# Sixty-four more tokens by gather and three dots ahead of a transpose, in a hybrid decoder block on one core

## The chip, the cores and the metric

The kernel runs on one core of one Trainium2 chip. The metric is the device time of one execution in microseconds (us), taken as the median of several runs. The hardware profiler records one further execution, and all rows of the trace come from it. The engines are named as the profile names them: PE is TensorE (PEld its weight loads), DVE is VectorE, ACT is ScalarE, POOL is GpSimd, SP is SyncE. A q behind the name means the engine's sequencer or queue.

## What is computed

One decoder block over 1024 tokens of width 1024: an RWKV-7 branch and a sparse attention branch are merged, then comes the PEER expert mixer, to which the change belongs. Each token has 8 heads; each head scores two sets of 128 sub-keys, takes the best 16 of each, and the best 16 of their sums. So a token has 128 slots, each with one of 16,384 experts and a gate. Cut to this part:

```python
s = einsum('thcn', q, sub_keys); s1, i1 = top_k(s[:, :, 0], 16); s2, i2 = top_k(s[:, :, 1], 16)
top_s, pos = top_k(s1[..., :, None] + s2[..., None, :], 16)      # 16 experts of each of 8 heads
experts = (i1 * 128 + i2)[pos]; gates = softmax(top_s)
act = gelu(einsum('cd,chkd->chk', h2, u_tab[experts])) * gates    # u_tab, v_tab: 16384 x 1024
y2  = einsum('chk,chkd->cd', act, v_tab[experts])
x   = layer_norm(ALPHA * x + gt2 * y2, ln2_g, ln2_b)
```

## The kernel before

The PEER stage treats the tokens in two ways. **Dense tokens** (the last DN = 640) go through all 16,384 experts: 128 groups of 128 experts (index i1) are multiplied with the tokens' h2, the result goes through Gelu and is multiplied by a gate table that is zero where a token has not chosen the expert, and the products go through the second table. **Gathered tokens** (the first TD = 384, three tiles of 128, one token to a partition) fetch only their own experts' rows from HBM, one slot of all 128 tokens per indirect DMA: 128 rows of 4 KB, 512 KB in one gather step. A tile has 128 steps on table u (a product and sum on DVE, L1389, gives one dot) and 128 on table v (a multiply and add into PSUM, L1393). Three tiles are 768 steps, called rows 0 to 767 below.

- `dots_u` (L1290) is one u group of the dense tokens. `split2` (L1265) loads a 512 KB weight tile (raw), ACT copies its high part (whi), POOL computes the low part (wlo, L1271); `mm6` (L1281) multiplies with both halves of the tokens, 48 matmuls of 320 columns in all (L1284, L1286, L1288). `dense_v` (L1319) does the same for table v. There are 128 u tiles and 136 v tiles (the last eight are read twice, for tokens 0 to 383 and 384 to 639 of the dense ones, each followed by a final layer norm, `fin1`, L1445).
- 69 of the u tiles are multiplied early, while keys are still being searched (`dots_ahead`, L1642); their results go to DRAM (dotD). The last part of the program multiplies the other 59 and all 136 v tiles.
- `retrieve` (L1118) finds the keys of one tile of 128 tokens, mostly on DVE. `by_slot` (L1228) transposes what it found on PE (L1233, into slots), and `gate_table` (L1240) writes the gate table of a dense tile in 16 blocks of 8 tokens: two compares on DVE, 8 scaled copies on ACT, 8 matmuls on PE (L1258), two copies.
- `peer_gather` (L1349) is the sequence of gather steps of a tile, `finish` (L1424) its residual and layer norm. Rows 0 to 127 are issued in the second merge and before, rows 128 to 299 beside the early dots, rows 300 on (MIDDLE) beside the rest. From row 300 on a step has one of four buffers (three named g, one g2); `finish` takes four more tiles of the name g for a tile that is not the last.

Each engine works through its instructions in one fixed order. That order is decided when the program is built, by a scheduler with a model of the machine, not written out by hand; a gather step of POOL waits until DVE has used the step four before it, and a DVE instruction that waits for a gather holds all that stands behind it on DVE.

Of the kernel before, what the change touches and what calls it, by code (L numbers as in the profile page):

```python
# [42 lines left out]
XOB = 2  # L43
QIB = 2
GM = 1
GX = 3
TIES = 3
ROW0 = 8
ROW1 = 128
NG = 3  # L50
TD = NG * 128
DN = 1024 - TD
CUT = 384
PAIRS = 3
# [148 lines left out]
def body(tc, a, out, dbg=None, ntiles=8, mark=lambda s: None):  # L203
# [227 lines left out]
    for H in range(2):  # L431
# [11 lines left out]
    xaD = [tc.dram_tile([128, 1024], F32, name=f"xaD{i}") for i in range(NG)]  # L443
    h2D = [tc.dram_tile([128, 1024], F32, name=f"h2D{i}") for i in range(NG)]
    xaT = tc.dram_tile([128, 8, DN], F32, name="xaT")

    def split_act(hi, lo, src):
# [556 lines left out]
    def merge(H, y, bz, mp, side, ties):  # L1004
# [75 lines left out]
        if c0 < 512:  # L1080
            for n in range(2):
                G.dma_start(h2TD[:, n, :, dst], h2T[:, n, :, c0:])
        for tt, xn in enumerate(xns[:max(0, NG - 4 * H)]):

            i = H * 4 + tt
            for n, to in enumerate((xaD[i], h2D[i])):
                o = mp.tile([128, 1024], F32, name="xo", bufs=XOB)
                V.tensor_tensor(o, xn, rows[2 * n], op=OP.mult)
                G.tensor_tensor(o, o, rows[2 * n + 1], op=OP.add)
                nc.sync.dma_start(to, o)  # L1090
# [27 lines left out]
    def retrieve(i, keysT, tp_, then):  # L1118
# [95 lines left out]
        if i < NG:  # L1214
            ef = i1
# [65 lines left out]
    def mm6(pts, wh, wl, ah, al, k, last, halves=HALVES):  # L1281
# [3 lines left out]
        for n, h in enumerate(halves):  # L1285
            mm(pts[n], lhsT=wh, rhs=al[:, h], start=False, stop=False)  # L1286
        for n, h in enumerate(halves):
            mm(pts[n], lhsT=wl, rhs=ah[:, h], start=False, stop=last)  # L1288

    def dots_u(i1, du, h2T, bufs):  # L1290
        uh, ul = split2(du, a["ut"][i1])
# [50 lines left out]

    def gather_all(at):

        for i in range(NG):
            acc = yield from peer_gather(i, at)
            finish(i, acc, at)

    def peer_gather(i, at):  # L1349

        pg = at["pg"]

        def index(row):
            t = (gp if row < EARLY else at["du"] if row < MIDDLE else at["dv"]).tile([128, 128], U32, name="gidx")
            nc.sync.dma_start(t, idxD[i])
            return t

        def room(row):
            if EARLY <= row < MIDDLE and row % (GB + GX) >= GB:
                return at["sl"].tile([128, 1024], F32, name="gx", bufs=GX)  # L1360
# [6 lines left out]
        nc.sync.dma_start(gates, gateD[i])  # L1367
        h2 = gp.tile([128, 1024], F32, name="gh2")
        nc.sync.dma_start(h2, h2D[i])
        if i > 0:  # L1370
            hp = pg.tile([128, 1024], F32, name="pg")
            copy(hp, h2)
            h2 = hp
        dots = gp.tile([128, 128], F32, name="dots")
        for n in range(4):

            half = slice(64 * (n % 2), 64 * (n % 2) + 64)
            if n == 2:
                acc = pg.tile([128, 1024], F32, name="pg")
            for k in range(half.start, half.stop):  # L1380
                row = 64 * (4 * i + n) + k - half.start
                if idx is None or row in (EARLY, MIDDLE):
                    idx = index(row)
                u = room(row)
                G.indirect_dma_start(out=u, out_offset=None, in_=a["u" if n < 2 else "v"],  # L1385
                                     in_offset=bass.IndirectOffsetOnAxis(ap=idx[:, k:k + 1], axis=0))
                with behind(row):
                    if n < 2:
# [6 lines left out]
            if n < 2:  # L1395
# [27 lines left out]

    def finish(i, acc, at):  # L1424

        last = i == NG - 1
# [3 lines left out]
        V.tensor_tensor(y2, acc, row, op=OP.mult)  # L1430
        nc.sync.dma_start(xa, xaD[i])
        V.tensor_tensor(y2, y2, xa, op=OP.add)
# [4 lines left out]
        out_rows(i * 128, 128, (y2[:, 0:512], y2[:, 512:1024]), y2, g, b, gp.tile([128, 16], F32, name="lnst"), last)  # L1437

    def fin_rows(du):
        ln, dst = (du.tile([128, 2, 1024], F32, name="gt", bufs=2) for _ in range(2))  # L1440
# [20 lines left out]

    slots = {}

    def by_slots(i, f):
        if i >= NG:
            slots[i] = tk.tile([128, 3, 128], F32, name="slots", bufs=2)
            by_slot(f, slots[i])

    qTD = [tc.dram_tile([128, 8, 512], F32, name=f"qTD{i}") for i in range(2)]
    h2TD = tc.dram_tile([128, 2, 8, DN], F32R, name="h2TD")  # L1470
# [15 lines left out]
    for H in range(2):  # L1486
# [127 lines left out]
    with tc.tile_pool(reuse_waits=REUSE, name="du", bufs=1) as du, \  # L1614
# [6 lines left out]
        with tc.tile_pool(reuse_waits=REUSE, name="slots", bufs=1) as sl, \  # L1621
# [8 lines left out]
                    by_slots(i, f)  # L1630
                found[i] = gate_table(i, slots[i], sl, du, st, keys8)

            for i in slots:
                table(i)
            side = retrieve_all(range(M1, 8), tk, table)
            more = {"du": du, "sl": sl, "pg": pg}
            rows = gather_all(more)
# [9 lines left out]
                    yield  # L1647

            ahead_ = dots_ahead()

            def beside(tables, dots, n):

# [81 lines left out]
```

## Time and profile before

| what | value |
|---|---|
| median of 3 runs | 3749.42 us (3740.57 to 3751.53) |
| the profiled execution's own time | 3743.65 us |
| its span, first to last instruction | 3741.9 us |
| PE busy | 3505.2 us (94%) |
| DVE, ACT, POOL busy | 2596.4 (69%), 1695.7 (45%), 1981.3 us (53%) |
| moved by the DMA engines | 920.95 MB, mean 246 GB/s |

The span is the time between the first and the last instruction; the profiled execution's own time is 1.75 us longer. Matmuls are pipelined, so their durations overlap, and the distance between starts tells the pace. The granted clock (PEclk) is the share of full speed that TensorE got. From 1677 us on PE works on the dense tokens, first with the gate tables between the dots, then without.

### The profile page before, as it was taken

What the parts mean: (1) busy time and instruction counts of PE and PEld (TensorE: products, weight loads), DVE (VectorE), ACT (ScalarE), POOL (GpSimd) and SP (SyncE); (2) the same over time, 40 slices, a digit from 0 to 9 for tenths busy, and PEclk for the clock granted to TensorE, in tenths of its full rate; (3) what the DMA queues carried; (4) which work ended last, traced back from release to release, by engine and by line L of the source; (5) the groups of instructions that cost most, each with busy time, mean ns of one, the idle gap of its engine ahead of it and who ended that gap; (6) DMA issues with size and microseconds to landing.
All of it is one profiled execution on the core that took longest, in us unless ns stands there. A gap on an engine that the chain in (4) does not pass through costs nothing.

```text
span 3741.9 us, 64784 instructions
## 1 busy us (share of the span) xinstructions
PE 3505.2 (94%) x24045; PEld 3139.0 (84%) x24045; DVE 2596.4 (69%) x5433; ACT 1695.7 (45%) x3230; POOL 1981.3 (53%) x1572
## 2 busy tenths in 40 slices
PE   8999999889999999869999999999999999999997
PEld 7677777666677777649999989999999999999997
DVE  7756653857467775899999985376777767676754
ACT  3549953243344443447667678322223322222223
POOL 5452222354455553245655532467677667677755
PEclk9999999989999999889999999999999999999998
DMA  7463323864676666378988864898999989989963
GB/s 231 137 171 103 107 87 123 290 196 161 214 220 219 215 212 218 115 250 317 335 308 316 309 240 171 292 333 322 334 330 331 323 319 327 340 320 325 333 225 123
DMA packets 436880, 920.95 MB, mean 246 GB/s; under 512 B 36452, under 2 KB 195508, under 8 KB 433876
## 3 DMA queue, kind: packets, MB, share of 16 engines
q1 hardware_dynamic: 311956, 498.38, 39.8%
q0 software_dynamic: 124608, 418.43, 31.4%
q8 instruction: 189, 3.10, 0.3%
q14 instruction: 127, 1.04, 0.1%
HBM read 791.59 MB, written 125.08 MB: 245 GB/s over the span
## 4 chain that ended last, share of the span: by engine, by line
PE 49%; DVE 14%; DMA 13%; issue 8%; POOL 7%; ACT 6%; SPq 0%; POOLq 0%; ACTq 0%; DVEq 0%
PE pair L1284 7%; PE pair L1286 7%; PE pair L1288 7%; PE acc L423 4%; PE acc L424 4%; PE acc L425 4%; POOL g L1385 3%; DMA g<-in_u_dram,gidx 3%; DMA raw<-in_vt_dram 3%; POOL wlo L1271 3%; DMA g<-in_v_dram,gidx 3%; PE tp L1258 2%; DMA raw<-in_ut_dram 2%; ACT gt L232 2%; PE acc L975 2%
## 5 line engine op out<-in xcount | busy, mean ns | idle before, releaser
L1271 POOL TENSOR_TENSOR wlo<-raw,whi 128x1024 fp32r<-128x1024 f32 x264 | 643.8, 2440 | 388.9 <-ACT whi L232 367.5
L413 POOL TENSOR_TENSOR wlo<-wraw,whi 128x512 fp32r<-128x512 f32 x280 | 371.3, 1329 | 557.3 <-ACT whi L232 505.9
L232 ACT ACTIVATE whi<-raw 128x1024 fp32r<-128x1024 f32 x264 | 278.9, 1057 | 681.1 <-PE pair L1286 320.7
L1385 POOL DMA_INDIRECT g<-in_u_dram,gidx x361 | 373.6, 1035 | 298.4 <-DVE g L1389 180.5
L1284 PE MATMUL pair<-A,whi 128*128 128x320 f32 (+2 forms) x2048 | 482.1, 312 | 25.6 <-DVE A L1316 18.3
L1393 DVE SCALAR_TENSOR_TENSOR pg<-g,dots,pg 128x1024 f32<-128x1024 f32 x317 | 407.1, 1284 | 123.1 <-DMA g<-in_v_dram,gidx 118.0
L1286 PE MATMUL pair<-A,whi 128*128 128x320 f32 (+2 forms) x2048 | 481.2, 311 | 0.2 <-DVE A L1316 0.2
L1288 PE MATMUL pair<-A,wlo 128*128 128x320 f32 (+2 forms) x2048 | 480.4, 311 | 0.6 <-POOL wlo L1271 0.6
L1288 PE MATMUL pair<-h2T,wlo 128*128 128x320 f32 x2048 | 474.3, 312 | 2.1 <-POOL wlo L1271 2.1
L1284 PE MATMUL pair<-h2T,whi 128*128 128x320 f32 x2048 | 475.6, 312 | 0.2 <-ACT ds L232 0.2
L1286 PE MATMUL pair<-h2T,whi 128*128 128x320 f32 x2048 | 473.3, 311 | 0.0
L1385 POOL DMA_INDIRECT g<-in_v_dram,gidx x320 | 307.7, 961 | 170.8 <-DVE pg L1393 80.8
L423 PE MATMUL acc<-big,whi 128*128 128x512 f32 x864 | 356.5, 413 | 18.6 <-DVE zs L531 6.8
L1284 PEld LDWEIGHTS pair<-A,whi 128*128 128x128 f32 x2048 | 349.1, 190 | 28.2 <-issue 19.1
L1389 DVE SCALAR_TENSOR_TENSOR g<-g,pg 128x1024 f32<-128x1024 f32 x233 | 281.0, 1216 | 118.4 <-DMA g<-in_u_dram,gidx 116.8
L425 PE MATMUL acc<-big,wlo 128*128 128x512 f32 x864 | 351.6, 407 | 2.3 <-POOL wlo L413 2.3
L424 PE MATMUL acc<-big,whi 128*128 128x512 f32 x864 | 349.5, 404 | 3.1 <-DVE big L449 3.1
L1288 PEld LDWEIGHTS pair<-A,wlo 128*128 128x128 f32 x2048 | 349.1, 190 | 0.8 <-POOL wlo L1271 0.8
L1286 PEld LDWEIGHTS pair<-A,whi 128*128 128x128 f32 x2048 | 349.2, 190 | 0.7 <-DVE A L1316 0.7
L1288 PEld LDWEIGHTS pair<-h2T,wlo 128*128 128x128 f32 x2048 | 343.8, 189 | 3.5 <-POOL wlo L1271 2.6
L1284 PEld LDWEIGHTS pair<-h2T,whi 128*128 128x128 f32 x2048 | 344.6, 189 | 1.6 <-ACT ds L232 0.4
L1286 PEld LDWEIGHTS pair<-h2T,whi 128*128 128x128 f32 x2048 | 343.9, 189 | 1.0
(482 smaller groups left out, 6682.5 us busy)
## 6 DMA issues: line engine op xcount, KB each, us to landing
raw<-in_vt_dram SPq DMA_DIRECT2D x136, 512.0 KB
raw<-in_ut_dram SPq DMA_DIRECT2D x128, 512.0 KB
gtD<-st SPq DMA_DIRECT2D x20, 2048.0 KB
gt<-gtD SPq DMA_DIRECT2D x32, 1280.0 KB
wraw<-in_wz_dram SPq DMA_DIRECT2D x152, 256.0 KB
dotD<-ds SPq DMA_DIRECT2D x69, 320.0 KB
al<-dotD SPq DMA_DIRECT2D x69, 320.0 KB
mw<-in_wada_dram SPq DMA_DIRECT2D x32, 512.0 KB
```

Of the source, the lines that this page charges most:

```text
L232: copy = lambda o, i, **k: A.activation(o, i, AF.Copy, **k)
L413: G.tensor_tensor(lo, raw, hi.bitcast(F32), op=OP.subtract)
L423: mm(pt, lhsT=wh[:, ks], rhs=ah[:, k, :], start=k == 0, stop=False)
L424: mm(pt, lhsT=wh[:, ks], rhs=al[:, k, :], start=False, stop=False)
L425: ins = mm(pt, lhsT=wl[:, ks], rhs=ah[:, k, :], start=False, stop=k == nk - 1)
L1271: G.tensor_tensor(lo, raw, hi.bitcast(F32), op=OP.subtract)
L1284: mm(pts[n], lhsT=wh, rhs=ah[:, h], start=k == 0, stop=False)
L1286: mm(pts[n], lhsT=wh, rhs=al[:, h], start=False, stop=False)
L1288: mm(pts[n], lhsT=wl, rhs=ah[:, h], start=False, stop=last)
L1385: G.indirect_dma_start(out=u, out_offset=None, in_=a["u" if n < 2 else "v"], in_offset=bass.IndirectOffsetOnAxis(ap=idx[:, k:k + 1], axis=0))
L1389: V.scalar_tensor_tensor(u, u, 1.0, h2, op0=OP.mult, op1=OP.mult, accum_out=dots[:, k:k + 1])
L1393: V.scalar_tensor_tensor(acc, u, dots[:, k:k + 1], acc, op0=OP.mult, op1=OP.add)
```

## The change

Sixty-four tokens (number 384 to 447, the first half of tile 3) are gathered instead of dense. DN becomes 576, so a dense matmul has 288 columns instead of 320 (and 384 and 192 instead of 384 and 256 in the last eight v tiles read twice). The 64 tokens take two partitions each, with 64 slots in each, so their gather is 64 steps on u and 64 on v, all on 128 partitions: 896 rows instead of 768. `finish` adds the two partitions of a token with a matmul against a 0/1 matrix. Tile 3's gate table has 8 blocks instead of 16. XR takes the place of the old constant GX (three early buffers).

Beside that, what the second merge finds for tile 3 is kept (`keep`) and not transposed there; the transposes are put behind three dots (FIRST). Cut to its core:

```diff
+FIRST = 3
+XR = 3
-TD = NG * 128
+GX = 64
+TD = NG * 128 + GX
+NGT = NG + (GX > 0)
...
-        for tt, xn in enumerate(xns[:max(0, NG - 4 * H)]):
+        for tt, xn in enumerate(xns[:max(0, NGT - 4 * H)]):
...
-        for b in range(16):
+        for b in range(max(0, TD - i * 128) // 8, 16):
...
-        for i in range(NG):
+        for i in range(NGT):
             acc = yield from peer_gather(i, at)
             finish(i, acc, at)
...
+        tokens = 128 if i < NG else GX
+        slots_ = tokens
+        halves = 2 if i < NG else 1
...
-        for n in range(4):
+        for n in range(2 * halves):
...
+            sel = gp.tile([128, 1024], F32, name="gh2")[:, 0:n]
+            V.tensor_reduce(sel, ident.rearrange("p (s t) -> p t s", t=n), axis=AX.X, op=OP.add)
+            copy(y2, acc)
+            acc = at["pg"].tile([128, 1024], F32, name="pg")
+            for h in range(2):
+                hs = slice(512 * h, 512 * h + 512)
+                mm(acc[p, hs], lhsT=sel, rhs=y2[:, hs], start=True, stop=True)
...
-                side = retrieve_all(range(1, M1), tk, by_slots)
+                side = retrieve_all(range(1, M1), tk, keep)
...
-            for i in slots:
-                table(i)
...
             ahead_ = dots_ahead()
+
+            for _ in range(FIRST):
+                next(ahead_)
+            for i, f in early_found.items():
+                with tc.issue_after(latest[0].ins):
+                    by_slots(i, f)
+                table(i)
```

On PE, where the last matmuls of the second merge (acc) are followed by the transposes of tile 3 (tp<-ident), stood before:

```order
L425 MATMUL acc<-Q,wlo 128x512
L1233 MATMUL tp<-ident,i_15675 128x128
L1233 MATMUL tp<-ident,gates 128x128
L1233 MATMUL tp<-ident,i_15674 128x128
L1128 MATMUL tp<-keysT,qT 128x128 x4
L1284 MATMUL pair<-h2T,whi 128x320 x2
```

and at the two ends of the same place stands now (L428 is the old L425, L1287, L1289 and L1291 are the dots, L1236 the transposes):

```order
L428 MATMUL acc<-Q,wlo 128x512
L1287 MATMUL pair<-h2T,whi 128x288 x2
L1289 MATMUL pair<-h2T,whi 128x288 x2
...
L1291 MATMUL pair<-h2T,wlo 128x288 x2
L1236 MATMUL tp<-ident,i_15685 128x128
L1236 MATMUL tp<-ident,gates 128x128
L1236 MATMUL tp<-ident,i_15684 128x128
L1131 MATMUL tp<-keysT,qT 128x128 x2
```

The three transposes moved behind 71 rows of dots, that is behind the 144 matmuls of three weight tiles.

On DVE the program ended before with the layer norm of the last dense tokens; its last gather step (L1393) stood 39 rows ahead of the end, among the last dense products (yacc):

```order
L1393 SCALAR_TENSOR_TENSOR pg<-g_36500,dots,pg 128x1024
L1330 SCALAR_TENSOR_TENSOR yacc<-pair,modc,yacc 128x640 x3
...
L1330 SCALAR_TENSOR_TENSOR yacc<-pair,modc,yacc 128x256 x7
L1404 BN_STATS lnst<-pair 128x6 x4
L1405 BN_AGGR lnst<-lnst 128x2 x2
L1407 RECIPROCAL lnst<-lnst 128x1 x2
L1410 SCALAR_TENSOR_TENSOR lnst<-lnst 128x1 x2
L1414 TENSOR_TENSOR gt<-gt 128x512 x4
```

Now the layer norm of the last dense tokens (L1426) is followed by gather steps: 9 of table v for tile 2, then tile 2's `finish` (L1445 and on), 64 of table u (L1401), the Gelu's product (L1409), 64 of table v (L1405) and the last `finish`:

```order
L1426 TENSOR_TENSOR gt<-gt 64x512 x2
L1405 SCALAR_TENSOR_TENSOR pg<-g_36306,dots,pg 128x1024
L1405 SCALAR_TENSOR_TENSOR pg<-g,dots,pg 128x1024 x3
...
L1445 TENSOR_TENSOR gacc<-pg,g 128x1024
L1457 TENSOR_TENSOR gacc<-gacc,g 128x1024
...
L1401 SCALAR_TENSOR_TENSOR g,dots<-g,pg 128x1024 x3
...
L1409 TENSOR_TENSOR dots<-dots,ggate 128x64
L1403 TENSOR_SCALAR pg<-g,dots 128x1024
```

137 gather steps moved behind the last instruction of the dense tokens, where there was none.

On POOL, between the low parts of two weight tiles in the middle of the last stage (g from in_u_dram are gather steps), stood before:

```order
L1271 TENSOR_TENSOR wlo<-raw,whi 128x1024
L1385 DMA g<-in_u_dram,gidx 128x1024 x3
L1271 TENSOR_TENSOR wlo<-raw,whi 128x1024
L1385 DMA g_35799<-in_u_dram,gidx 128x1024
L1385 DMA g<-in_u_dram,gidx 128x1024 x2
L1271 TENSOR_TENSOR wlo<-raw,whi 128x1024
```

and stands now:

```order
L1274 TENSOR_TENSOR wlo<-raw,whi 128x1024
L1397 DMA g_35617<-in_u_dram,gidx 128x1024
L1397 DMA g<-in_u_dram,gidx 128x1024
L1274 TENSOR_TENSOR wlo<-raw,whi 128x1024
L1397 DMA g<-in_u_dram,gidx 128x1024 x2
L1274 TENSOR_TENSOR wlo<-raw,whi 128x1024
```

Counted over all rows of POOL from weight tile 80 to weight tile 240, 441 gather steps stood there before (319 to 760) and 382 stand there now (313 to 695): 2.76 and 2.39 for each weight tile. The last eight v tiles that are read twice (16 tiles, 249 to 264) had no gather step beside them; now 35 DVE gather steps stand among their products and layer norms.

## Rows read from the trace of the kernel before

**Rows 1.** Busy time by stage: length, busy us (instructions) by engine, clock, DMA share, GB/s.

```profile
1640.00:1677.00 37.00, 5.99 (x29) 4.37 (x27) 31.79 (x86) 10.52 (x14) 19.93 (x18) 0.60 0.86 302
1677.00:2384.00 707.00, 681.00 (x4850) 667.02 (x4851) 573.00 (x1298) 496.33 (x1009) 356.06 (x237) 0.99 0.78 284
2384.00:3616.00 1232.00, 1211.84 (x8190) 1209.21 (x8189) 865.47 (x1055) 345.01 (x423) 851.77 (x638) 0.99 0.91 325
3657.00:3736.00 79.00, 63.52 (x425) 62.60 (x423) 38.45 (x62) 27.01 (x35) 48.76 (x25) 0.91 0.34 117
```

**Rows 2.** Waits of PE, 2420 to 3660 us: us in total, times, longest.

```profile
PE pair L1284 <- DVE A L1316: 18.3, 8, 4.3
```

**Rows 3.** Timeline of DVE: start, us, operation [idle before]; last gather step, last instructions.

```profile
3615.05 1.28 DVE L1393 SCALAR_TENSOR_TENSOR pg<-g,dots,pg 128x1024 f32<-128x1024 f32 x1
...
3731.00 4.70 DVE L1414 TENSOR_TENSOR gt<-gt 128x512 f32<-128x512 f32 x4 [0.76 <-ACT gt L1413]
```

**Rows 4.** Timeline of PE: matmuls of 320 columns, the first of 384, two of 256.

```profile
3628.70 0.46 PE L1284 MATMUL pair<-h2T,whi 128*128 128x320 f32 x2
...
3656.86 0.34 PE L1284 MATMUL pair<-A,whi 128*128 128x384 f32 x1
...
3702.05 0.29 PE L1284 MATMUL pair<-A,whi 128*128 128x256 f32 x1
...
3704.94 0.28 PE L1284 MATMUL pair<-A,whi 128*128 128x256 f32 x1
```

**Rows 5.** Busy time by stage of line L1258 alone: PE, PEld, then as in Rows 1.

```profile
1677.00:2384.00 707.00, 161.70 (x1280) 154.21 (x1280) 0.99 0.78 284
```

**Rows 6.** Timeline of PE: the transposes of tile 3 and the first dot.

```profile
1674.93 0.45 PE L1233 MATMUL tp<-ident,i 128*128 128x128 f32 x1 [31.01 <-DVE i L1193]
...
1676.89 0.90 PE L1284 MATMUL pair<-h2T,whi 128*128 128x320 f32 x2
```

**Rows 7.** Timeline of POOL: load of h2T, low parts of the first two weight tiles.

```profile
1654.72 2.79 POOL L1618 DMA_DIRECT2D h2T<-h2TD  x4 [1.00 <-issue]
1657.53 4.64 POOL L1271 TENSOR_TENSOR wlo<-raw,whi 128x1024 fp32r<-128x1024 f32 x2
```

**Rows 8.** DMA, 1650 to 1675 us, eight loads and six gather steps of POOL among it.

```profile
DMA packets 3677, 9.82 MB, mean 393 GB/s; under 512 B 290, under 2 KB 546, under 8 KB 3676
```

**Rows 9.** Timeline of POOL in the first merge: one add of xo.

```profile
763.50 2.38 POOL L1089 TENSOR_TENSOR xo<-xo,big 128x1024 f32<-128x1024 f32 x1 [6.10 <-DVE xo L1088]
```

**Rows 10.** Groups on DVE, 2384 to 3742 us: busy us, mean ns, idle before by releaser.

```profile
L1393 DVE SCALAR_TENSOR_TENSOR pg<-g,dots,pg 128x1024 f32<-128x1024 f32 x254 | 326.4, 1285 | 122.4 <-DMA g<-in_v_dram,gidx 118.0 <-DVE pg L1393 0.7 <-DVE A L1316 0.6
L1389 DVE SCALAR_TENSOR_TENSOR g<-g,pg 128x1024 f32<-128x1024 f32 x212 | 256.0, 1216 | 117.5 <-DMA g<-in_u_dram,gidx 115.9
```

**Rows 11.** Timeline of POOL: two gather steps after a pause.

```profile
3595.68 0.95 POOL L1385 DMA_INDIRECT g<-in_v_dram,gidx  x1
3596.93 0.94 POOL L1385 DMA_INDIRECT g<-in_v_dram,gidx  x1 [0.30 <-issue]
```

**Rows 12.** Timeline of DVE: the use of the first of these two.

```profile
3600.38 1.29 DVE L1393 SCALAR_TENSOR_TENSOR pg<-g,dots,pg 128x1024 f32<-128x1024 f32 x1 [3.09 <-DMA g<-in_v_dram,gidx]
```

**Rows 13.** Timeline of DVE around the finish of tile 1, inside the dense stretch.

```profile
2944.35 1.29 DVE L1393 SCALAR_TENSOR_TENSOR pg<-g,dots,pg 128x1024 f32<-128x1024 f32 x1 [0.71 <-DMA g<-in_v_dram,gidx]
...
2967.49 1.22 DVE L1389 SCALAR_TENSOR_TENSOR g<-g,pg 128x1024 f32<-128x1024 f32 x1
```

**Rows 14.** Timeline of DVE: from a last u step to the next step, past Gelu.

```profile
2444.03 1.22 DVE L1389 SCALAR_TENSOR_TENSOR g<-g,pg 128x1024 f32<-128x1024 f32 x1
...
2448.24 1.21 DVE L1389 SCALAR_TENSOR_TENSOR g<-g,pg 128x1024 f32<-128x1024 f32 x1
```

**Rows 15.** Timeline of DVE and POOL: begin and end of the last finish.

```profile
3660.85 1.22 DVE L1430 TENSOR_TENSOR gacc<-pg,A 128x1024 f32<-128x1024 f32 x1
...
3674.43 1.30 POOL L1415 TENSOR_TENSOR gacc<-gacc,gt 128x512 f32<-128x512 f32 x1 [0.63 <-DVE gacc L1414]
```

**Rows 16.** Timeline of POOL: the last instruction before the last store.

```profile
3731.77 6.26 POOL L1415 TENSOR_TENSOR gt<-gt 128x512 f32<-128x512 f32 x4 [10.08 <-DVE gt L1414]
```

More of the change, by code (lines that the diff above doesn't have):

```diff
@@ L45 @@
 GM = 1
-GX = 3
+FIRST = 3
+XR = 3
 TIES = 3
@@ L442, in body @@
         ybD[H] = tc.dram_tile([8, 128, 512], F32, name=f"ybD{H}")
-    xaD = [tc.dram_tile([128, 1024], F32, name=f"xaD{i}") for i in range(NG)]
-    h2D = [tc.dram_tile([128, 1024], F32, name=f"h2D{i}") for i in range(NG)]
+    xaD = [tc.dram_tile([128, 1024], F32, name=f"xaD{i}") for i in range(NGT)]
+    h2D = [tc.dram_tile([128, 1024], F32, name=f"h2D{i}") for i in range(NGT)]
     xaT = tc.dram_tile([128, 8, DN], F32, name="xaT")
@@ L1213, in retrieve @@
         V.tensor_tensor(gv, gv, gs[:, :, None].to_broadcast([128, 8, 16]), op=OP.mult)
-        if i < NG:
-            ef = i1
+        if i < NGT:
+            ef = i1 if i < NG else tp_.tile([128, 128], F32, name="ef")
             V.scalar_tensor_tensor(ef, i1, 128.0, i2, op0=OP.mult, op1=OP.add)
@@ L1287, in mm6 @@
         for n, h in enumerate(halves):
-            mm(pts[n], lhsT=wl, rhs=ah[:, h], start=False, stop=last)
+            latest[:] = [mm(pts[n], lhsT=wl, rhs=ah[:, h], start=False, stop=last)]
     def dots_u(i1, du, h2T, bufs):
@@ L1343, in gather_all, with rows_in @@
     def gather_all(at):
-        for i in range(NG):
+        for i in range(NGT):
             acc = yield from peer_gather(i, at)
             finish(i, acc, at)
+    def rows_in(dst, src, n, c):
+        for r in range(128 // n):
+            at = 0 if src.shape[1] == c else r * c
+            nc.sync.dma_start(dst[r * n:r * n + n, 0:c], src[0:n, at:at + c])
     def peer_gather(i, at):
         pg = at["pg"]
+        tokens = 128 if i < NG else GX
+        slots_ = tokens
+        halves = 2 if i < NG else 1
         def index(row):
             t = (gp if row < EARLY else at["du"] if row < MIDDLE else at["dv"]).tile([128, 128], U32, name="gidx")
-            nc.sync.dma_start(t, idxD[i])
+            rows_in(t, idxD[i], tokens, slots_)
             return t
         def room(row):
-            if EARLY <= row < MIDDLE and row % (GB + GX) >= GB:
-                return at["sl"].tile([128, 1024], F32, name="gx", bufs=GX)
+            if EARLY <= row < MIDDLE and row % (GB + XR) >= GB:
+                return at["sl"].tile([128, 1024], F32, name="gx", bufs=XR)
             if row >= MIDDLE and row % (GB + GM) >= GB:
@@ L1366, in peer_gather @@
         gates = gp.tile([128, 128], F32, name="ggate")
-        nc.sync.dma_start(gates, gateD[i])
+        rows_in(gates, gateD[i], tokens, slots_)
         h2 = gp.tile([128, 1024], F32, name="gh2")
-        nc.sync.dma_start(h2, h2D[i])
+        rows_in(h2, h2D[i], tokens, 1024)
         if i > 0:
@@ L1374, in peer_gather @@
         dots = gp.tile([128, 128], F32, name="dots")
-        for n in range(4):
-            half = slice(64 * (n % 2), 64 * (n % 2) + 64)
-            if n == 2:
+        for n in range(2 * halves):
+            half = slice(0, slots_) if halves == 1 else slice(64 * (n % 2), 64 * (n % 2) + 64)
+            if n == halves:
                 acc = pg.tile([128, 1024], F32, name="pg")
@@ L1384, in peer_gather @@
                 u = room(row)
-                G.indirect_dma_start(out=u, out_offset=None, in_=a["u" if n < 2 else "v"],
+                G.indirect_dma_start(out=u, out_offset=None, in_=a["u" if n < halves else "v"],
                                      in_offset=bass.IndirectOffsetOnAxis(ap=idx[:, k:k + 1], axis=0))
                 with behind(row):
-                    if n < 2:
+                    if n < halves:
                         V.scalar_tensor_tensor(u, u, 1.0, h2, op0=OP.mult, op1=OP.mult, accum_out=dots[:, k:k + 1])
@@ L1394, in peer_gather @@
                 yield
-            if n < 2:
+            if n < halves:
                 A.activation(dots[:, half], dots[:, half], AF.Gelu)
@@ L1424, in finish @@
     def finish(i, acc, at):
-        last = i == NG - 1
+        last = i == NGT - 1
+        n = 128 if i < NG else GX
+        p = slice(0, n)
         row, xa = ((at["dv"].tile([128, 2 * DN], F32, name="A", bufs=AB)[:, 0:1024] if last else grow()) for _ in range(2))
@@ L1429, in finish @@
         y2 = gp.tile([128, 1024], F32, name="gacc")
-        V.tensor_tensor(y2, acc, row, op=OP.mult)
-        nc.sync.dma_start(xa, xaD[i])
-        V.tensor_tensor(y2, y2, xa, op=OP.add)
+        if n == 128:
+            V.tensor_tensor(y2, acc, row, op=OP.mult)
+        else:
+            sel = gp.tile([128, 1024], F32, name="gh2")[:, 0:n]
[5 more added lines that the diff above has]
+                mm(acc[p, hs], lhsT=sel, rhs=y2[:, hs], start=True, stop=True)
+            V.tensor_tensor(y2[p], acc[p], row[p], op=OP.mult)
+        nc.sync.dma_start(xa[p], xaD[i][p])
+        V.tensor_tensor(y2[p], y2[p], xa[p], op=OP.add)
         g, b = at["ln"][0:2] if last else (grow(), grow())
@@ L1436, in finish @@
             rowb(b, "ln2b")
-        out_rows(i * 128, 128, (y2[:, 0:512], y2[:, 512:1024]), y2, g, b, gp.tile([128, 16], F32, name="lnst"), last)
+        out_rows(i * 128, n, (y2[:, 0:512], y2[:, 512:1024]), y2, g, b, gp.tile([128, 16], F32, name="lnst"), last)
     def fin_rows(du):
@@ L1462, in body @@
     slots = {}
+    early_found = {}
     def by_slots(i, f):
@@ L1467, in by_slots, with keep @@
             by_slot(f, slots[i])
+    def keep(i, f):
+        if i >= NG:
+            early_found[i] = f
     qTD = [tc.dram_tile([128, 8, 512], F32, name=f"qTD{i}") for i in range(2)]
```

## The prediction

> **What bounds the kernel now.** I read the busy time by stage first [rows 1]. There the reader is to see that from 1677 us on PE hardly rests: 681.0 of 707 us while the keys are searched and the gate tables built, 1211.8 of 1232 us beside the gather steps, at a granted clock of 0.99. The DMA share in the long stretch is 0.91, with 325 GB/s, so the transfers are close behind PE. Then the waits of PE in that stretch: only 18.3 us in all go to products that come late from DVE [rows 2]. Then the end of DVE's timeline: the last gather step starts at 3615.05 and the dense tokens' layer norm ends at 3731.00 + 4.70 = 3735.7 us [rows 3]. So gathering is done 120 us before the dense tokens, and whatever shortens PE's work before that point shortens the kernel, until the gather steps become the later of the two. The change pulls both ways: fewer columns on PE, 128 more gather steps.
>
> **What PE saves.** In the timeline of PE 192 matmuls of 320 columns lie between 3628.70 and 3656.86, so 146.7 ns each; 24 of 256 columns lie between 3702.05 and 3704.94, so 120.4 ns [rows 4]. No row has 288 columns. The two prices bound it; I take the middle, 133.5 ns, as 288 is the middle of 256 and 320. That saves 13.1 ns a matmul, 0.630 us for a weight tile of 48.
> - 69 early dots: 43.5 us. DVE would be the cover that fails here: it is busy 573 of 707 us [rows 1], and loses little, so it still fits into the 647 us that remain.
> - 59 other u tiles and 120 whole v tiles: 179 x 0.630 = 112.8 us.
> - The eight half tiles of 256 columns that now have 192: 192 matmuls by 26.2 ns, 5.0 us; 0 if a shorter matmul waits for its weights.
> - Eight blocks less of tile 3's table: L1258 has 1280 matmul records in 80 blocks and 161.7 us [rows 5], so 2.02 us a block, 16.2 us.
>
> **What the moved transposes save.** PE sat idle for 31.01 us until tile 3's keys were there at 1674.93, and the first dot started at 1676.89 [rows 6]. Three dots of 6.4 us could fill 19.2 us of it. But they need h2T, whose load POOL has issued by 1657.5, and low parts of weights, the second of which is ready at 1662.2 [rows 7]. The load is 5.2 MB and the DMA engines move 393 GB/s there [rows 8], so 13.3 us from 1651, and I expect the first dot near 1665: 12 us earlier, of which I count 10. The bounds are 0 (the dots wait for something else) and 19. Behind the transposes wait tile 3's table and the key matmuls of tile 4; they come later by the rest of the third dot, and DVE has gather steps to do meanwhile.
>
> **What is added ahead of the tail.** One more tile of xo in the first merge: two adds on POOL of 2.38 us [rows 9], with the weights' low parts queued behind them. Bounds 0 and 4.8; I take 2. The last double-read tiles, 79 us at 117 GB/s [rows 1] or 9.2 MB, get 35 gather steps beside them, 18.4 MB more. At 325 GB/s the 27.6 MB take 85 us, at 393 they take 70, against 74 of PE's work; I add 6 us (0 to 11). In the long stretch nothing is added: 2.39 gather steps now go with a tile of 6.41 us where 2.76 went with 7.04, so weights and gathers together ask for 277 GB/s where they asked for 280.
>
> The dense tokens would then end 43.5 + 112.8 + 5.0 + 16.2 + 10 - 2 - 6 = 179.5 us earlier, at 3556.2.
>
> **The tail, which is new.** 137 gather steps stand on DVE behind the last instruction of the dense tokens, so none of their DVE work can be hidden. One step costs DVE 1.285 us on table v and 1.216 on u [rows 10]. POOL issues two 1.25 us apart [rows 11]. A transfer of 524,288 bytes takes 1.33 us at 393 GB/s [rows 8]. So 1.33 us is the lower bound of a step. But there are four buffers, and the way round one of them is longer: 4.70 us from the issue at 3595.68 to the use at 3600.38 [rows 11, 12], 1.29 for the use, 0.30 until POOL issues again: 6.29 us, a quarter of which is 1.57 us. The upper bound is the pace of the long stretch, 468 steps in 1232 us [rows 1] or 2.63 us; but there the order ties the steps to the weight tiles. I take 1.57, because the row that it comes from has a weight load beside it and little else: 137 x 1.57 = 215.1 us.
> - Tile 2's finish now stands in the tail, with its four tiles named g. In tile 1's finish 23.14 us passed from the last v step at 2944.35 to the fourth u step at 2967.49 [rows 13]; less four steps of 1.57 that is 16.9 us.
> - Gelu between u and v: 4.21 us from the last u step to the next step [rows 14], less one step, say 3 us.
> - The last finish: 14.9 us from 3660.85 to the end of its last add [rows 15], partly shared with dense work, a copy and two matmuls for the pairs (2 us, estimated), and 3.9 us from POOL's last end at 3738.03 to the end of the span [rows 16]: 20 us.
>
> 215.1 + 16.9 + 3 + 20 = 255 us, so the span ends at 3811.2 instead of 3741.9, 69.3 us later. The profiled execution's own time was 3743.65, which gives 3813 us; that run lies 0.15% below the median of the runs shown, 3749.42. What PE saves comes back as a tail in which PE has nothing to do.
>
> **The rivals.** *A shorter way round.* With no weight load beside it a transfer may land sooner than 4.70 us after its issue, down to 1.33 us a step: 182.2 instead of 215.1 us, 3780 us in all. The early stage speaks for it, with 393 GB/s over 25 us [rows 8]; against it, that no gather there was used at once. A rule of the Trainium skill leads the same way: "DMA: Bandwidth & Descriptors", section "Anatomy of one DMA — SWDGE (gpsimd) path", fits a transfer from POOL's path as 2.0 us plus its bytes over 436 GB/s, 3.2 us for a gather step. With issue and use that would be an estimate of 1.44 us a step and 3795 us; the row's 4.70 us, less the issue of 0.95, is 3.75 and so above it.
>
> *A slower tail.* If a transfer of random rows keeps the way that it has beside the weights, the step stays at 2.0 to 2.63 us, 3872 to 3958 us. The 118 and 116 us for which DVE waited for gathers [rows 10] speak for it; that the order set the pace there speaks against. The same side takes the case that gathers hold PE up in the long stretch, since DVE's products stand behind them.
>
> *Faster.* PE's price falls by more than I think. To end 0.3% lower, at 3732 us, the dense tokens must end 81 us earlier still; over 248 whole tiles of 48 matmuls that is 6.8 ns each, so 288 columns would have to cost below 126.7 ns, near the 120.4 of 256. The tail alone can't do it: it would need steps of less than 1 us, and DVE alone needs 1.22.
>
> *The transposes bring nothing:* 10 us more, inside the range.
>
> **How the numbers follow.** My forecast (step of 1.45 to 1.75 us, 3797 to 3838) gets 0.62, the shorter way round 0.18, the slower tail 0.14, faster 0.03, no change 0.03 (a fast step and a larger gain together). A difference of 0.3%, 11 us, is about what a measurement of this kernel can tell from no change. The range leaves out the two last cases, most of the slower tail and the lowest edge of the short one: 3768 to 3862.
>
> **What would show it.** Right: dots of 288 columns 133 ns apart; PE's idle time before the transposes gone, dots from about 1665; the last product of the dense tokens near 3556; behind it some 250 us with PE almost idle, DVE's steps 1.5 to 1.7 us apart, each waiting for its gather, and POOL waiting for DVE. Wrong: PE waits of far more than 18 us for DVE's products in the long stretch (the gathers hold PE); steps 1.3 or 2 us apart in the tail; or a tail that starts much before or after 3556.

## The result, and the profile after

The changed kernel takes 3915.06 us (median of four runs, 3897.85 to 3920.95), the kernel before 3750.48 beside it: ratio 1.0433, interval 1.04 to 1.0465, so slower. The forecast was 3813 us, 3768 to 3862; slower came true, the size did not. The profiled execution took 3897.85 us with a span of 3895.7, 84.5 us behind the span that the prediction adds up to.

The page of the changed kernel: busy time, then DMA packets.

```profile
PE 3364.8 (86%) x23921; PEld 2994.4 (77%) x23921; DVE 2739.8 (70%) x5625; ACT 1650.8 (42%) x3156; POOL 2102.5 (54%) x1702
...
DMA packets 448418, 977.19 MB, mean 251 GB/s; under 512 B 42036, under 2 KB 190084, under 8 KB 445668
```

Busy time by stage, columns as in [rows 1]: a piece of the dense stretch, its end, two of the tail.

```profile
2600.00:2800.00 200.00, 198.38 (x1486) 197.82 (x1485) 139.61 (x143) 58.86 (x75) 141.92 (x104) 1.00 0.92 333
...
3500.00:3600.00 100.00, 81.72 (x501) 79.35 (x500) 69.60 (x81) 27.08 (x33) 82.23 (x61) 0.89 0.89 305
3600.00:3700.00 100.00, 6.68 (x50) 6.14 (x49) 74.98 (x105) 5.86 (x9) 52.48 (x54) 0.53 0.83 282
3700.00:3850.00 150.00, 0.00 (x0) 0.00 (x0) 105.86 (x119) 0.26 (x1) 77.80 (x84) 0.50 0.87 293
```

Up to 3500 us it looks like [rows 1]. Then comes the tail: PE has nothing to do and its granted clock stands at 0.5, the lower of the two levels; the DMA share is a little lower than beside the dense tokens, 0.83 to 0.87 in place of 0.92, and no other engine is full.

Timeline of POOL: the 301st, the 768th and the 896th, last gather. In the kernel before the 301st stands at 2384.50, the 768th and last at 3605.86.

```profile
2357.79 0.95 POOL L1397 DMA_INDIRECT g<-in_u_dram,gidx  x1 [7.17 <-DMA gidx<-idxD]
...
3631.71 0.94 POOL L1397 DMA_INDIRECT g<-in_v_dram,gidx  x1 [2.23 <-DVE pg L1405]
...
3868.05 0.94 POOL L1397 DMA_INDIRECT g<-in_v_dram,gidx  x1 [0.53 <-DVE pg L1405]
```

These rows give the time as one chain of gathers. From the 301st gather to the 768th are 467 steps: 1221.4 us before (2.615 each), 1273.9 after (2.728). Then 128 steps in 236.3 us (1.846 each, finish of tile 2 and Gelu included), then 27.6 us to the end of the span. The gathers, which were done 120 us ahead of the dense tokens [rows 3], now end last.

Timeline of DVE: the end of the dense tokens' last layer norm, which answers to the second row of [rows 3], with a v step behind it.

```profile
3617.90 5.20 DVE L1426 TENSOR_TENSOR gt<-gt 128x512 f32<-128x512 f32 x3
3623.02 3.92 DVE L1405 SCALAR_TENSOR_TENSOR pg<-g,dots,pg 128x1024 f32<-128x1024 f32 x3
```

3623.1 against 3735.7: 112.6 us earlier, where 179.5 were forecast.

PE's waits from 1650 to 2380 us, after; in the kernel before, the four that answer were 11.5, 0, 2.1 and, beside the single idle time of 31.0, 8.7.

```profile
PE tp L1261 <- ACT st L235: 21.9, 16, 3.7
PE pair L1287 <- ACT whi L235: 18.1, 3, 11.2
PE pair L1291 <- POOL wlo L1274: 17.2, 12, 3.8
PE tp L1236 <- DVE i L1196: 5.5, 3, 1.9
```

The tail itself on table u, POOL and then DVE: a gather, the step whose end freed its buffer, and the step that uses it.

```profile
3702.58 0.93 POOL L1397 DMA_INDIRECT g<-in_u_dram,gidx  x1 [1.83 <-DVE g L1401]
```
```profile
3701.08 1.22 DVE L1401 SCALAR_TENSOR_TENSOR g<-g,pg 128x1024 f32<-128x1024 f32 x1 [1.53 <-DMA g<-in_u_dram,gidx]
...
3708.06 1.22 DVE L1401 SCALAR_TENSOR_TENSOR g<-g,pg 128x1024 f32<-128x1024 f32 x1 [1.14 <-DMA g<-in_u_dram,gidx]
```

POOL waits for DVE to free a buffer, DVE for the gather to land, here 6.98 us for one way round, 5.48 of it from issue to use. The median over gathers 775 to 825, pairing the nth gather with the nth step, is 5.47; with 1.22 for the use and 0.28 until the next issue a buffer's way round is 6.97 us, a quarter of it 1.74, and the issues from the 775th to the 825th follow each other 1.733 us apart.

### The profile page after: what moved, and what is told of

It is laid out like the page before. It is cut to its first block, busy times and chain, and to the rows that moved or that the text cites. A ratio compares the mean times of both kernels' runs of the same rounds, so it can differ in the third digit from the quotient of the medians.

```text
span 3895.7 us, 65006 instructions
## 1 busy us (share of the span) xinstructions
PE 3364.8 (86%) x23921; PEld 2994.4 (77%) x23921; DVE 2739.8 (70%) x5625; ACT 1650.8 (42%) x3156; POOL 2102.5 (54%) x1702
## 5 line engine op out<-in xcount | busy, mean ns | idle before, releaser
L1397 POOL DMA_INDIRECT g<-in_u_dram,gidx x425 | 434.5, 1022 | 341.7 <-DVE g L1401 211.0
L1405 DVE SCALAR_TENSOR_TENSOR pg<-g,dots,pg 128x1024 f32<-128x1024 f32 x380 | 488.1, 1285 | 158.9 <-DMA g<-in_v_dram,gidx 146.9
L1287 PE MATMUL pair<-A,whi 128*128 128x288 f32 (+2 forms) x2048 | 460.3, 302 | 35.5 <-DVE A L1319 24.4
L1397 POOL DMA_INDIRECT g<-in_v_dram,gidx x384 | 365.8, 953 | 231.3 <-DVE pg L1405 128.3
L1401 DVE SCALAR_TENSOR_TENSOR g<-g,pg 128x1024 f32<-128x1024 f32 x297 | 358.3, 1216 | 161.4 <-DMA g<-in_u_dram,gidx 158.7
L1291 PE MATMUL pair<-h2T,wlo 128*128 128x288 f32 x2048 | 452.5, 301 | 17.2 <-POOL wlo L1274 17.2
L1287 PE MATMUL pair<-h2T,whi 128*128 128x288 f32 x2048 | 451.4, 301 | 18.3 <-ACT whi L235 18.1
L1291 PE MATMUL pair<-A,wlo 128*128 128x288 f32 (+2 forms) x2048 | 458.2, 301 | 4.8 <-POOL wlo L1274 4.8
L1289 PE MATMUL pair<-A,whi 128*128 128x288 f32 (+2 forms) x2048 | 458.4, 301 | 1.9 <-DVE A L1319 1.9
L1289 PE MATMUL pair<-h2T,whi 128*128 128x288 f32 x2048 | 447.7, 300 | 0.0
L1287 PEld LDWEIGHTS pair<-A,whi 128*128 128x128 f32 x2048 | 341.7, 193 | 39.1 <-issue 26.2
L1291 PEld LDWEIGHTS pair<-h2T,wlo 128*128 128x128 f32 x2048 | 335.6, 192 | 21.1 <-POOL wlo L1274 20.0
L1287 PEld LDWEIGHTS pair<-h2T,whi 128*128 128x128 f32 x2048 | 335.9, 192 | 20.7 <-ACT whi L235 19.1
L428 PE MATMUL acc<-big,wlo 128*128 128x512 f32 x864 | 349.4, 405 | 2.3 <-POOL wlo L416 2.3
L1291 PEld LDWEIGHTS pair<-A,wlo 128*128 128x128 f32 x2048 | 341.6, 193 | 5.5 <-POOL wlo L1274 5.5
L1289 PEld LDWEIGHTS pair<-A,whi 128*128 128x128 f32 x2048 | 342.0, 193 | 2.5 <-DVE A L1319 2.5
L1289 PEld LDWEIGHTS pair<-h2T,whi 128*128 128x128 f32 x2048 | 335.8, 192 | 0.7
```

What stands on the lines that cost most here:

```text
L428: ins = mm(pt, lhsT=wl[:, ks], rhs=ah[:, k, :], start=False, stop=k == nk - 1)
L1287: mm(pts[n], lhsT=wh, rhs=ah[:, h], start=k == 0, stop=False)
L1291: latest[:] = [mm(pts[n], lhsT=wl, rhs=ah[:, h], start=False, stop=last)]
```

## The experiments

All are compared with the kernel before on the same chip. Four kernels asked first whether PE's pace carries through.

**The move alone.**

```diff
-GX = 64
+GX = 0
```

> The move of the transposes alone: 384 tokens are gathered and 640 stay dense, as before the change; the last keys found in the second merge are transposed behind three dots. Theory of the prediction (up to the dense stage PE sets the pace, so what PE gains at the start of the early stage is kept to the end): the 10 to 24 us that PE gains at the first dots pass through, 3727 to 3740 us. Rival (the early stage ends with its last gate table, which follows DVE and ACT, so a gain of PE alone is lost in a wait ahead of the dense stage): no gain, 3745 to 3755 us.

3743.23 us, ratio 0.9985 (0.9971 to 0.9999): 6 us, between the two theories. The first dot starts at 1656.44 instead of 1676.89 [rows 6], but PE's last dense matmul is only 11 us earlier.

**The gathers alone.**

```diff
-FIRST = 3
+FIRST = 0
-                side = retrieve_all(range(1, M1), tk, keep)
+                side = retrieve_all(range(1, M1), tk, by_slots)
-            for i, f in early_found.items():
-                with tc.issue_after(latest[0].ins):
-                    by_slots(i, f)
+            for i in list(slots):
                 table(i)
```

> The 64 more gathered tokens alone: the transposes stay in the second merge's place, ahead of every dot. Theory of the prediction (PE's pace counts to the end): later than the changed kernel by what the move gave, 10 to 24 us, so 3920 to 3940 us. Rival (the early stage ends with the last gate table): the same as the changed kernel within 6 us, 3900 to 3921 us, and the wait ahead of the dense stage shorter by 10 to 24 us than the changed kernel's 38 us.

3907.25 us, 1.0421 (1.04 to 1.0441): the same as with the move. The first dot is 37 us later than in the changed kernel, PE's last dense matmul 6 us, and the time not at all. So the slowdown comes with the 64 tokens alone, and the move neither helps nor harms it.

**75 early dots instead of 69.** In the changed kernel the early dots run out at 2296 us, and until 2331 PE has only table matmuls, in lots that wait for ACT (14.2 us in all).

```diff
-EXTRA = 10
+EXTRA = 16
```

> The changed kernel with 75 dots computed ahead in place of 69. Rival (PE stands idle ahead of the dense stage because the early dots run out before the last gate table is written and read back): the six dots, some 30 us of PE at 48 matmuls each, fill the idle time of about 38 us and are missing later from the dense stage, so the dense stage ends 22 to 32 us earlier and the time is 3870 to 3893 us. Theory of the prediction (PE sets the pace throughout): the dots only change their place, 3898 to 3921 us.

3911.33 us, 1.0441 (1.0418 to 1.0464): no gain. This is the run that settles most. Its PE timeline shows where the dense tokens' transposes begin, 3605.20 in the changed kernel:

```profile
3570.97 0.71 PE L1477 MATMUL pair<-ident,yacc 128*128 128x128 f32 x5
```

No table matmul waits for ACT in this kernel from 2230 to 2360 us, and PE is done 34 us earlier, as the rival said, although this profile's first dot starts 9 us later (the changed kernel's profile is the shortest of its runs). But the time stays; the theory of the prediction has the time right and the reason wrong. The gathers end where they did: the 301st is issued at 2376.63, the 768th at 3630.89 and the last at 3873.85. The program's order, which is made anew for every version, now leaves 155 steps behind the last instruction of the dense tokens, where it left 137, so what PE gains only lengthens the tail.

**The move with 75 dots**, 384 tokens gathered.

```diff
-EXTRA = 10
+EXTRA = 16
-GX = 64
+GX = 0
```

> The move alone, 384 tokens gathered, with 75 dots computed ahead in place of 69. Rival (the move's gain is lost ahead of the dense stage where the early dots run out): the added dots give it back, 3722 to 3738 us, while the move with 69 dots stays at 3745 to 3755. Theory of the prediction: the same as the move with 69 dots, 3727 to 3740 us.

3742.11 us, 0.9973 (0.9959 to 0.9986): of the versions that compute every row the only one that, with the move alone, lies below both kernels, by 0.27%. It can't be told from the move alone, and its own profiled execution took 3751.27.

Next came the gathers.

**Two more buffers.**

```diff
-GM = 1
+GM = 3
```

> The changed kernel with six gather buffers in place of four from row 300 on. Theory A (a step of the last stretch lasts a quarter of the way from a gather's issue round to the buffer's next use, 5.3 to 6.3 us and more over four buffers): with six buffers a step comes below 1.5 us, and the 126 steps behind the last dense token give back 35 us or more, 3845 to 3880 us. Theory B (the DMA engines themselves pass one 512 KB gather in about 1.79 us, whatever stands in line): the step stays at 1.7 to 1.8 us, the time from issue to use grows to 8 us or more, 3895 to 3920 us.

3791.32 us, 1.0113 (1.009 to 1.0136): 124 us off, more than either theory allowed, on the side of theory A. Busy time of the gathers alone (POOL), in 1000 us beside the dense tokens and in 50 us of the tail: length, busy us (gathers), clock, DMA share, GB/s. The changed kernel:

```profile
2450.00:3450.00 1000.00, 340.68 (x362) 0.99 0.89 323
3700.00:3750.00 50.00, 25.95 (x28) 0.50 0.88 297
```

With six buffers, the tail once in the same 50 us and once behind the dense tokens' layer norm, which lasts to 3714 here:

```profile
2450.00:3450.00 1000.00, 391.76 (x415) 0.98 0.95 345
3700.00:3750.00 50.00, 30.87 (x33) 0.50 0.95 357
3720.00:3760.00 40.00, 28.34 (x31) 0.50 1.02 399
```

The tail alone shows theory A: the last 35 steps are 1.325 us apart, where four buffers took 1.73 to 1.80, and issue to use is 6.4 us, not the 8 and more of theory B. DVE rests no more; its timeline has 14 steps in 18.5 us:

```profile
3714.08 18.50 DVE L1405 SCALAR_TENSOR_TENSOR pg<-g,dots,pg 128x1024 f32<-128x1024 f32 x14
```

Beside the dense tokens there are 415 gathers in place of 362, but not by the buffers alone. With six buffers the program's order itself has 2.88 gather steps for each weight tile from tile 80 to tile 240, counted as in the section on the change, instead of 2.39; which of the two made the pace, no run separates. The last gather is issued 106 us sooner, at 3762.0. But PE now pays for it; its waits from 2460 to 3500 us, six buffers:

```profile
PE pair L1291 <- POOL wlo L1274: 40.1, 31, 2.6
PE pair L1287 <- ACT whi L235: 22.4, 14, 5.5
```

In the changed kernel the row that answers to [rows 2] leads, and no wait for weights is listed:

```profile
PE pair L1287 <- DVE A L1319: 22.1, 10, 4.4
```

So 62.5 us of waiting for weights, where there was none, and PE's last dense matmul comes at 3697 instead of 3605. Followed back to what came late, some 45 of the 62.5 us end at the load of a weight tile, and some 11 at gather steps that stand ahead of a low part on POOL.

**Without the fourth tile's gathers.**

```diff
-        for i in range(NGT):
+        for i in range(NG):
-        last = i == NGT - 1
+        last = i == NG - 1
```

> The changed kernel without the gathers of the fourth tile: the expert mixing of the 64 tokens and their 64 output rows are left out, 576 tokens stay dense, and 768 gathers remain. Theory of the prediction (PE sets the pace to the end of the dense tokens): 3565 to 3590 us. Rival (from the dense stage on, weights and gathers share the DMA engines, and the 768th gather is issued at 3630 us behind PE's end at 3605 us): the third tile's finish ends it, 3650 to 3680 us, so the 128 gathers of the fourth tile alone cost 230 to 260 us.

3667.14 us, 0.9784 (0.9764 to 0.9804). The 128 gathers cost 248 us, and with 768 gathers the fewer dense tokens give only 79 us against the kernel before (3746.54 beside it): the rival. PE is done at 3622, the last gather step at 3651.

**Sixty rows ahead of the dense stage**, in the stretch in which the DMA engines idle.

```diff
-MIDDLE = 300
+MIDDLE = 360
-            n = (MIDDLE - EARLY) // (steps + 6)
+            n = (300 - EARLY) // (steps + 6)
```

Rows 300 to 359 then also take the six early buffers (g and gx) of the rows ahead of them.

> The changed kernel with 60 more gathered rows (300 to 359) ahead of the dense stage, behind the last retrieval, where the DMA engines are busy for 0.54 of 2200 to 2300 us and no gather runs from 2218 to 2358 us. Theory of the gather stream (behind row 300 the end is the number of gathers left, each at its DMA time): up to 60 steps of 1.79 us are saved, less what the added DVE steps cost the last gate tables, 3800 to 3850 us. Theory of the prediction (the dense stage's end and then a tail): the 60 rows shorten the tail too, but the added DVE work holds up the tables that PE waits for, so 3830 to 3880 us.

3836.87 us, 1.024 (1.0221 to 1.0258), inside both forecasts. It saves 78 us although one row of PE shows what the added steps cost, the dense tokens' first products behind them on DVE:

```profile
2414.67 0.82 PE L1287 MATMUL pair<-h2T,whi 128*128 128x288 f32 x2 [43.35 <-DVE A L1319]
```

**All three together.**

```diff
-EXTRA = 10
+EXTRA = 16
-MIDDLE = 300
+MIDDLE = 360
...
-GM = 1
+GM = 3
...
```

The second mark stands for the line on n, as with the sixty rows, here and in all kernels below that change MIDDLE.

> The changed kernel with the three edits together: 60 rows ahead of the dense stage, six gather buffers from there on, 75 dots computed ahead. Theory of the gather stream with the DMA engines as its limit: no better than the 60 rows alone within 10 us, 3790 to 3850 us, since dots and buffers move no byte. Theory A (buffers limit the last stretch): 40 us or more below the 60 rows alone. In neither is it below the kernel before at 3750 us.

3796.24 us, 1.0112 (1.0087 to 1.0137). That is 41 us below the sixty rows alone, as theory A wanted, but no better than the two buffers alone, so rows and dots add nothing to them; the first product is again 35.1 us late.

**Five buffers and seven.**

```diff
-GM = 1
+GM = 2
```

> The changed kernel with five gather buffers from row 300 on (four gave 3915 us, six 3791). Theory A (the way round a buffer over the number of buffers sets the step): a step of the last stretch goes from 1.8 us to about 1.45, of the dense stretch from 2.78 to about 2.5, and the time lies between, 3825 to 3865 us. Theory A with the DMA engines' limit met already at five: 3785 to 3810 us.

3852.41 us, 1.0269 (1.0252 to 1.0287), in the range of theory A. Gathers alone, five buffers:

```profile
2450.00:3450.00 1000.00, 351.19 (x372) 1.00 0.91 329
3700.00:3750.00 50.00, 31.11 (x34) 0.50 0.96 347
```

In the tail 34 gathers in place of 28: steps of 1.52 us, between the 1.73 to 1.80 of four buffers and the 1.325 of six. The DMA share of 0.96 looked like a limit and was none, for the sixth buffer brought 399 GB/s in place of 347.

```diff
-GM = 1
+GM = 4
```

> The changed kernel with seven gather buffers from row 300 on. If the DMA engines are the limit at six (they were busy for 0.95 to 0.98 of the dense stretches, and a gather's way from issue to use had grown from 7.1 to 11 us): no better than six, 3775 to 3805 us, the way longer again by about a sixth. If buffers still set the step: 20 us or more below six, 3735 to 3770 us.

3794.44 us, 1.0122 (1.0102 to 1.0142): no better than six, as the DMA engines' limit would have it. Gathers alone, and then PE's waits from 2460 to 3500 us, seven buffers:

```profile
2450.00:3450.00 1000.00, 409.35 (x434) 0.95 0.95 347
```
```profile
PE pair L1291 <- POOL wlo L1274: 64.8, 54, 3.6
PE pair L1287 <- ACT whi L235: 43.9, 15, 8.7
```

The DMA share and the rate are those of six; 19 more gathers come through in 1000 us (3.34 steps a weight tile in the program's order), and PE waits 108.7 us for weights, some 66 of them for a load. The gathers are done at 3724, PE at 3775: the last place has changed hands, and the time has not.

**Six buffers without the fourth tile's gathers.**

```diff
-GM = 1
+GM = 3
-        for i in range(NGT):
+        for i in range(NG):
-        last = i == NGT - 1
+        last = i == NG - 1
```

> Six gather buffers and no gathers of the fourth tile: the expert mixing of the 64 tokens and their output rows are left out. The gathers then end near 3510 us and PE's end sets the time. Theory of the prediction (the dense stage is PE's alone): 3580 to 3615 us, some 55 to 85 below the four buffers without the fourth tile at 3667. Rival (weights and gathers share the DMA engines, and faster gathers hold up the weights by some 60 us): 3640 to 3680 us, so the dense tokens' saving of 180 us doesn't come through even without a tail.

3686.34 us, 0.9821 (0.9798 to 0.9844): the rival, a little beyond its range, and above the 3667 of four buffers. The gathers end at 3517, PE at 3672 after waits of 67.3 us for weights.

**Thirty and 42 rows ahead, with six and seven buffers.**

```diff
-MIDDLE = 300
+MIDDLE = 330
...
-GM = 1
+GM = 3
...
```

> The changed kernel with six gather buffers and 30 more rows ahead of the dense stage (sixty made the first dense product 35 to 43 us late). If the 30 rows only fill the idle DMA engines ahead of the dense stage: 30 steps of 1.6 to 2.4 us less, 3725 to 3765 us. If their DVE steps hold up the first dense product as sixty rows did: 3775 to 3800 us, no better than six buffers alone.

3756.68 us, 1.0027 (1.0011 to 1.0043): the best with 448 tokens gathered, 35 us below six buffers alone and 8 us above the kernel before. Busy time by stage ahead of the dense tokens, columns as in [rows 1]; first the kernel with five buffers and no added rows (the buffers differ only behind row 300), then this one:

```profile
2200.00:2350.00 150.00, 134.82 (x999) 130.90 (x997) 103.70 (x232) 118.06 (x247) 47.71 (x26) 0.95 0.56 206
```
```profile
2200.00:2350.00 150.00, 128.25 (x931) 124.55 (x931) 126.14 (x262) 115.69 (x240) 76.28 (x54) 0.94 0.78 286
```

12 MB more pass there (80 GB/s over 150 us), and no late product shows.

```diff
-MIDDLE = 300
+MIDDLE = 342
...
-GM = 1
+GM = 3
...
```

> The changed kernel with six gather buffers and 42 more rows ahead of the dense stage (30 gave 3757 us, 35 less than six buffers alone, with no wait at the first dense product; 60 with six buffers and 75 early dots gave 3796, with a wait of 35 us there). If what counts is the bytes that pass while the DMA engines would stand idle: 12 steps of 1.1 us less, 3738 to 3752 us, below the kernel before. If the added DVE steps already make the first dense product late: 3755 to 3775 us.

3782.78 us, 1.0084 (1.0067 to 1.0101), above both expectations. The first product is 9.5 us late, and behind it the DMA share is 0.92 where it was 0.94 with 30 rows; why so little lateness should cost 26 us the rows don't tell.

```diff
-MIDDLE = 300
+MIDDLE = 330
...
-GM = 1
+GM = 4
...
```

> Thirty rows ahead of the dense stage and seven buffers in place of six. If the DMA engines are the limit behind 2350 us, as six and seven buffers without the rows say (3791 and 3794): no change from 3757, 3748 to 3766 us. If the buffers still set the step once the rows are ahead: 3725 to 3745 us.

3790.26 us, 1.011 (1.0089 to 1.0132), above both again, since I had thought that the seventh buffer could at worst do nothing. The gathers end at 3683 and PE at 3768, after 109 us of waits for weights: on the reading below, the buffer takes DMA time from the chain that is now the later one.

## Why the prediction was wrong

**Right.** Fewer columns: from tile 72 to tile 248 the changed kernel's lead over before grows from 35.9 to 140.4 us, 0.594 us for each of 176 weight tiles where 0.630 were forecast. The transposes wait for nothing at their new place, the first dot starts at 1652.43 (I had expected 1665, with a load of 5.2 MB, which is that of 640 tokens; 576 have 4.7), and behind the dense tokens stands a tail in which DVE waits for gathers and POOL for DVE.

**The step that failed first is the dense tokens' end, 179.5 us earlier at 3556.2.** It came 112.6 us earlier. Three parts are missing. By tile 72 the sum had 10 - 2 + 72 x 0.630 + 16.2 = 69.6 us and 35.9 came: I took 681 of 707 us [rows 1] for a stage that PE sets and asked of DVE only whether its 573 us fit in, but dots that are shorter and start sooner run out before the last table, which goes at the pace of DVE and ACT. More early dots showed that, for they took the lump away. The long stretch gave 104.5 instead of 110.9. And the last double-read stretch, whose whole change I had at 5.0 - 6 = 1 us lost, lost 28, 20 of them on PE. Beside gather steps its matmuls wait for weights (9.5 us), and PE, which rests more, has less of its clock. Busy time by stage, columns as in [rows 1], before and then after:

```profile
3657.00:3725.00 68.00, 61.70 (x411) 61.03 (x410) 30.02 (x47) 23.75 (x29) 44.53 (x22) 0.95 0.40 136
```
```profile
3516.00:3605.00 89.00, 70.72 (x418) 68.35 (x417) 61.09 (x73) 22.27 (x26) 73.20 (x55) 0.87 0.88 299
```

PE stands idle for 18.3 us instead of 6.3, and the granted clock is 0.87 instead of 0.95. The other 8 us pass between the last dense matmul and the end of the layer norm. That last part is read from the trace alone; no run tests it.

**What a gain on PE is worth** the prediction also had wrong: whatever shortens PE's work was to shorten the kernel until the gathers are the later. The sum, a tail behind an end that PE sets, closes for the changed kernel, where 137 steps do stand behind that end. But it holds for this one order: the run with more early dots gave PE 34 us and the time nothing, because 155 steps stood behind. Beside the dense tokens the order gives the gathers so many steps for each weight tile. Counted from tile 80 to tile 240 (PE's time for a tile):

| kernel | steps for a tile | us for a tile | us for a step |
|---|---|---|---|
| before | 2.76 | 7.20 | 2.61 |
| changed, four buffers | 2.39 | 6.61 | 2.77 |
| 75 early dots, four buffers | 2.36 | 6.50 | 2.75 |
| five buffers | 2.46 | 6.59 | 2.68 |
| six | 2.88 | 7.01 | 2.44 |
| seven | 3.34 | 7.59 | 2.27 |

So the step is longer after than before because fewer steps are written for a tile, and the tile's time falls by less. That the order ties the steps to the weight tiles, as the prediction had it, these counts don't contradict. The buffers are not tight there as a rule: issue to use took 6.8 to 7.1 us before (median of gathers 500 to 699 and 310 to 499), the use 1.2 to 1.3, and 1.2 passed until the next issue, 1.7 after, where the tail has 0.28. Whether the buffers would change the pace in one and the same order was not run.

**The term of the tail, 137 x 1.57 us, was mis-sized.** Measured from the dense tokens' end to the span's end: 272.6 us instead of 255. Steps took 1.80 us on table u and 1.79 on v, since issue to use was 5.47 and not 4.70: I had taken [rows 11, 12] from the first gather after a pause, with nothing in line ahead of it. The next one, issued at 3596.93, was used 5.76 us later:

```profile
3602.69 1.29 DVE L1393 SCALAR_TENSOR_TENSOR pg<-g,dots,pg 128x1024 f32<-128x1024 f32 x1 [1.02 <-DMA g<-in_v_dram,gidx]
```

And [rows 10] showed DVE waiting for gathers as a rule. That the way round a buffer sets the tail's step the runs with five and six buffers show: 1.52 and 1.325 us. The offsets were too large: 9.0 us from the last v step of tile 2 (3636.60) to the next u step, instead of 16.9 [rows 13] plus one step; Gelu 1.95 (from 3758.73), instead of 3 [rows 14] plus a step. The last finish was right: 21 us from the last step's end. The steps were more than 25 us too cheap, and the offsets gave some 11 of that back. So 66.9 from the dense tokens' end and 17.6 from the tail make the 84.5.

**The rivals.** The slower tail, 3872 to 3958 us, holds the result, but not by its mechanism, steps of 2 us and more. The Trainium skill's fit in "DMA: Bandwidth & Descriptors", section "Anatomy of one DMA — SWDGE (gpsimd) path", leads to an estimate of 1.44 us a step and is further off than the row was: 5.47 us less 0.95 for the issue is 4.5 us a transfer, against its 3.2. The fit is for one transfer, and four are under way here.

**What stands behind the buffers** in the dense stretch is, as far as the runs go, the DMA engines' rate, which weights and gathers share. With six or seven buffers the rate is 345 and 347 GB/s, PE waits for weights, and whether PE or the gathers end last, the time is 3791 and 3794 us. That is argued, not shown: the weights have two buffers (raw), which no run changed. The same page of the Trainium skill, section "Issuing engines are not separate DMA queues", says that transfers from all issuers run on the same 16 engines and interleave; the trade of 62.5 and 108.7 us of PE's waits for 53 and 72 more gathers agrees. That page of the Trainium skill, section "Where 436 GB/s comes from", puts the memory's share of a core at about 358 GB/s. The 345 to 347 lie near it, but it's no ceiling here: the six buffers' tail ran at 399 GB/s for 40 us, and 25 us of the kernel before at 393 [rows 8]. Moving bytes into the idle time ahead of the dense tokens is what gained beyond that, up to the point where it made their products late.

**Open.** What the scheduler goes by when it writes fewer or more steps for a weight tile; whether a third raw buffer would take PE's waits away; why 42 rows lose 26 us to 30. Whether fewer bytes (the early dots and tables go through memory and back) would bring 448 gathered tokens below 384 was not tried.

## What to carry to other kernels

When work is moved from one chain to another that looks hidden, count in the order as built how many steps stand beside the longer chain and how many behind it, and count again for every version: a gain on one chain is not to be subtracted from the total. A ring of buffers sets a pace by its way round over their number, and that way is to be read in the middle of a run with the ring full, not at the first step behind a pause. Another buffer helps as long as the rate in GB/s still rises, which the DMA share doesn't tell; then it takes from the loads that another engine waits for.

## What the runs showed of the hardware that was not expected

With more gathers in line each one takes longer. Median issue to use in the dense stretch (gathers 500 to 699): 7.0 us with four buffers, 9.6 with five, 10.6 with six, 11.9 with seven. In the tail, with no weights beside them, 5.5 with four, 6.0 with five and 6.4 with six, while the step falls: 1.73 to 1.80 us with four, 1.52 with five, 1.325 with six, where DVE, with 1.29 us for each use, goes from one to the next. The DMA share there is 0.88, 0.96 and 1.02 at 297, 347 and 399 GB/s: at 0.96 there was still 15% more to come.
